# Attention trunk on one core: compressed scores kept in PSUM until their row minimum is subtracted

## The chip, the core and the metric

The kernel runs on one core of a Trainium2 chip. The metric is the device time of one execution in microseconds (us). The engines are named as in the profile: PE (TensorE, matrix products and transposes), ACT (ScalarE, activations and copies), DVE (VectorE, elementwise operations and reductions), POOL (GpSimd, elementwise operations, and it issues some DMAs), SP (it issues most DMAs).

## The reference

One layer of a decoder trunk over 512 positions of width 1024, in float32. A pooling mixer and a sparse attention with 16 heads of 64, in two key groups, are merged by gates and followed by a squared-ReLU MLP. The attention has three branches; the change touches the first, in which every query attends to 31 compressed keys per group:

```python
k_cmp = compress(kc.reshape(B, S, G, dh), pe_k, w_ck1, w_ck2)
v_cmp = compress(vc.reshape(B, S, G, dh), pe_v, w_cv1, w_cv2)
...
s_c = jnp.einsum('bqghd,bngd->bghqn', qb, k_cmp) * scale
p_c = masked_softmax(s_c, cmp_end[None, :] <= t[:, None])
o_c = jnp.einsum('bghqn,bngd->bqghd', p_c, v_cmp)
...
s_s = jnp.einsum('bqghd,bgqkd->bghqk', qb, k_sel) * scale
p_s = masked_softmax(s_s, ok[:, :, None])
...
o = gb[..., 0:1] * o_c + gb[..., 1:2] * o_s + gb[..., 2:3] * o_w
```

The other two branches (selected blocks, sliding window) are causal attention over all keys at these sizes, with keys of their own.

## The kernel before

Every float32 product is made of three products of rounded parts (high and low), so PE does about three times the plain work. The span has three stages: projections and the pooling mixer (to about 182 us), attention (about 182 to 390 us), and the output projections and the MLP.

**The attention stage.** Heads are worked in eight pairs. A pair has twelve slots: four in which both dense branches of one block of 128 queries are done together (`half == 0`), and eight with one branch each. Keys are negated beforehand, so the softmax works with a minimum and `exp(-x)`. A loop runs over all slots, each with steps for several engines:

- `score_pe` (L1013, PE): the scores of one slot, into a PSUM bank of the tag "S", which has three banks (`S_BANKS = 3`). `psS` is its name.
- `smax` (L1035, DVE): adds the mask, writes `P` in SBUF, takes the row minimum into `sm`.
- `expo` (L1045, ACT): the exponential, with row sums.
- `weight` (L1055 on DVE, a reciprocal; L1058 on POOL): scales `P` by reciprocal and gate.
- `turn_pe` (L1075, PE), four slots later: transposes `P` into a PSUM bank of the tag "T", of which there are two. `turn_hi` (L1086, ACT) and `turn_lo` (L1090, DVE) split it into `PT`.
- `pv` (L1109, PE): the product with the values. `o_evac` (L1116, L1118) takes it out.

**Compressed scores.** `cmp_scores(p)` does the compressed branch of the pair `p`, one pair ahead, as a generator whose steps run between the slots. Its PSUM tile `psC` is also one of the three "S" banks. Eight small products (L950) fill it: for each of 8 rows (4 query blocks x 2 heads) 32 high and 32 low columns. DVE adds the mask to the high part (L957) and the low part to that (L958), both into the SBUF tile `cw`; it takes the minimum over each row (L960) and subtracts it (L962), `cw` from `cw`. ACT takes the exponential (L965), DVE sum and reciprocal (L967, L968, L970), POOL scales and splits (L972, L974, L975), PE transposes (L983), ACT copies to `pc` (L985).

**Work between.** `fill2` does the remaining projections in `fm` (L394, PE). Their weights are split into a high part by ACT (L351) and a low part by DVE or POOL (L353). Queries are rotated in `rope`: ACT copies the projection to `rx` (L618), SP issues four DMAs that make `rs`, the same with halves swapped (L621), POOL multiplies both by tables (L626, L629), DVE adds them (L634), and `q_done` splits the sum into `Q` (L659 to L664).

**The order.** The source gives an emission order; a scheduler then orders the instructions of each engine by its own estimates of times, and puts semaphore waits in. Banks of a tag are handed out in turn: the tile that is asked for third after `psC` gets the bank of `psC`, and has to wait for the last reader of `psC`. That tile is the second of two scores 512 wide (128 queries x 512 keys) in a pair.

Of the kernel before, what the change touches and what calls it, by code (L numbers as in the profile page):

```python
# [16 lines left out]
ALU = mybir.AluOpType  # L17
AX = mybir.AxisListType
# [44 lines left out]
def trunk(ctx: ExitStack, tc: tile.TileContext, A, out):  # L63
    nc = tc.nc
    PE, ACT, DVE, POOL = nc.tensor, nc.scalar, nc.vector, nc.gpsimd
    PSUM = bass.MemoryType.PSUM

    def pool(name, **kw):
        return tc.tile_pool(name=name, bufs=1, reuse_waits="tile", **kw)
# [409 lines left out]
    op = e2.enter_context(pool("op"))  # L479
# [410 lines left out]
    with ExitStack() as c2:  # L890
# [54 lines left out]
        def cmp_scores(p):  # L945
            g = p // 4
            ps = ps2.tile([128, NT, 2, 64], F32, tag="S", bufs=S_BANKS, name="psC")
            for qb in range(NT):
                for h in range(2):
                    PE.matmul(ps[:, qb, h, :], Q[p][:, h, 128 * qb:128 * qb + 128], KC[g], start=True, stop=True,  # L950
                              skip_group_check=True)
            w = p2.tile([128, NT, 2, 64], F32, tag="cw", bufs=1, name="cw")
            s8 = p2.tile([128, 3, 8], F32, tag="c8", bufs=1, name="c8")
            cm = cst[:, C_CM:C_CM + 128].rearrange("p (q n) -> p q n", q=NT)
            wl = w[:, :, :, 0:32]
            wf = w.rearrange("p q h n -> p (q h) n")[:, :, 0:32]
            DVE.tensor_tensor(wl, ps[:, :, :, 0:32], cm[:, :, None, :].to_broadcast([128, NT, 2, 32]), op=ALU.add)  # L957
            DVE.tensor_tensor(wl, ps[:, :, :, 32:64], wl, op=ALU.add)  # L958
            yield
            DVE.tensor_reduce(s8[:, 0, :], wf, axis=AX.X, op=ALU.min)  # L960
            yield
            DVE.tensor_tensor(wf, wf, s8[:, 0, :, None].to_broadcast([128, 8, 32]), op=ALU.subtract)  # L962
            yield
            yield
            ACT.activation(wl, wl, AF.Exp, scale=-1.0)  # L965
            yield
            DVE.tensor_reduce(s8[:, 1, :], wf, axis=AX.X, op=ALU.add)  # L967
            DVE.reciprocal(s8[:, 2, :], s8[:, 1, :])  # L968
            r = s8[:, 2, :].rearrange("p (q h) -> p q h", q=NT)
            DVE.tensor_tensor(r, r, GT[:, :, 6 * p:6 * p + 6:3], op=ALU.mult)  # L970
            yield
            POOL.tensor_tensor(wl, wl, r[:, :, :, None].to_broadcast([128, NT, 2, 32]), op=ALU.mult)  # L972
            pH, pL = (PC[:, :, e, :].rearrange("p q (h n) -> p q h n", h=2) for e in range(2))
            POOL.tensor_scalar(pH, wl, 1.0, 1.0, op0=ALU.mult, op1=ALU.mult)  # L974
            POOL.tensor_tensor(pL, wl, pH.bitcast(F32), op=ALU.subtract)  # L975
            yield
            yield
            yield
            yield
            pt = ps2.tile([128, S], F32, tag="T", bufs=T_BANKS, name="psT")  # L980
            for qb in range(NT):
                src = PC[:, qb, :, :].rearrange("p e c -> p (e c)")
                PE.transpose(pt[:, 128 * qb:128 * qb + 128].bitcast(FR), src, identR)  # L983
            t = p2.tile([128, S], FR, tag="pc", bufs=1, name="pc")
            ACT.activation(t, pt, AF.Copy)  # L985
            PTc[p] = t
# [126 lines left out]
        def o_evac(p, half):  # L1113
# [7 lines left out]
            split_ready()  # L1121

        side.append(cmp_scores(0))
        while 0 not in PTc:
            fill()
            step_side()
        n = len(slots)
# [4 lines left out]
        for i in range(n + LAG + PLAG):  # L1132
            if i < n:
                p = slots[i][0]
                if i % 12 == 3 and p + 1 < NPAIR:
                    while p + 1 not in Q:
                        fill()
                        step_side()
                if i % 12 == CMP_AT and p + 1 < NPAIR:
                    side.append(cmp_scores(p + 1))  # L1140
# [51 lines left out]
    def bank():  # L1192
        return ps3.tile([128, S], F32, tag="B", bufs=8, name="psB")
# [396 lines left out]
    ps = [bank() for _ in range(2)]  # L1590
# [15 lines left out]
    for t in (2, 3):  # L1606
        n = 512 if t == 2 else 256
        for c in range(0, 512, n):
            ps = bank()[:, 0:n]
# [42 lines left out]
```

## Time and profile before

| | us |
|---|---|
| median of 3 runs | 816.5 (815.71 to 817.32) |
| profiled execution, its own time | 814.65 |
| span of the profiled execution | 812.9 |
| PE busy | 788.6 (97%) |
| DVE busy | 627.4 (77%) |
| ACT busy | 491.6 (60%) |
| POOL busy | 207.8 (26%) |

The span lies within the execution's time; 1.75 us of it are outside the span. Busy shares are means over stages that differ, so stages are read by themselves. In a row of the timeline the first number is the start, the second the time that the row covers, `x3` that three like instructions follow one another, and the brackets tell how long the engine was idle before it and what ended that. The granted clock (PEclk) is 1.00 at full speed.

### The profile page before, as it was taken

The numbers are of one execution on the slowest core, as the hardware profiler recorded it, in microseconds if no ns is written. First come the engines' busy times: TensorE is split into PE (matmuls) and PEld (weight loads), VectorE is DVE, ScalarE is ACT, GpSimd is POOL, SyncE is SP. The second block draws the span as 40 slices with busy tenths as digits, with TensorE's granted clock in tenths as the row PEclk, the third lists the DMA queues.
The fourth block names the chain that finished last, engine by engine and source line by source line (L and its number), as shares of the span: only waits on it lengthen the run. The fifth ranks groups of instructions, "written<-read, shape, count | busy, mean of one in ns | idle before, by whom it ended". The sixth has DMA issues, their size and how long they took to land.

```text
span 812.9 us, 14154 instructions
## 1 busy us (share of the span) xinstructions
PE 788.6 (97%) x5163; PEld 710.2 (87%) x5163; DVE 627.4 (77%) x1217; ACT 491.6 (60%) x968; POOL 207.8 (26%) x273
## 2 busy tenths in 40 slices
PE   8999999998899999999999999999999999999996
PEld 7889878886788888888788899999999999999996
DVE  5796744539879898889664579996889688978975
ACT  6576533337777888899434466943773477347833
POOL 4000000028766867665334100111111110000000
PEclk9999999999999999999999999999999999999999
DMA  9554633357446634553964707999998997754522
GB/s 304 143 158 122 164 92 94 102 170 153 67 124 122 144 79 92 104 131 65 328 152 154 202 9 208 311 243 283 250 286 218 285 266 194 222 164 156 181 79 104
DMA packets 128752, 136.65 MB, mean 168 GB/s; under 512 B 5349, under 2 KB 117001, under 8 KB 128522
## 3 DMA queue, kind: packets, MB, share of 16 engines
q1 hardware_dynamic: 107274, 113.98, 43.5%
q0 software_dynamic: 21120, 20.97, 18.1%
q8 instruction: 41, 0.67, 0.3%
q10 hardware_dynamic: 288, 0.79, 0.3%
q14 instruction: 29, 0.24, 0.1%
HBM read 131.01 MB, written 44.04 MB: 215 GB/s over the span
## 4 chain that ended last, share of the span: by engine, by line
PE 73%; DVE 16%; ACT 6%; issue 3%; DMA 1%; POOL 1%; ACTq 0%; DVEq 0%; POOLq 0%
PE psF L394 22%; PE psB L1379 15%; PE psB L394 12%; PE psB L1498 9%; PE psO L1109 3%; PE psT L1075 3%; PE psS L1013 2%; DVE wl L308 2%; PE psV L394 2%; DVE P L1035 2%; DVE PT L1090 1%; PE psF L451 1%; ACT P L1045 1%; DVE w3l L308 1%; PE psC L714 1%
## 5 line engine op out<-in xcount | busy, mean ns | idle before, releaser
L394 PE MATMUL psF<-R,wh 128*128 128x512 f32 x512 | 166.8, 404 | 0.9 <-ACT GB L688 0.6
L306 ACT ACTIVATE wh<-raw 128x1024 fp32r<-128x1024 f32 x70 | 74.0, 1057 | 74.5 <-PE psB L1498 32.6
L351 ACT ACTIVATE wh<-raw 128x512 fp32r<-128x512 f32 (+1 forms) x100 | 60.2, 620 | 82.2 <-PE psF L394 37.4
L394 PEld LDWEIGHTS psF<-R,wh 128*128 128x128 f32 x512 | 92.5, 189 | 18.7 <-ACT GB L688 0.8
L273 POOL DMA_DIRECT2D S<-w_ff x40 | 46.3, 1158 | 233.0 <-DMA S<-w_ff 162.5
L394 PE MATMUL psF<-R,wl 128*128 128x512 f32 x256 | 101.9, 398 | 0.8 <-DVE wl L353 0.8
L1058 POOL TENSOR_SCALAR P<-P,sm,GT 128x128 f32<-128x128 f32 (+3 forms) x128 | 85.7, 702 | 47.9 <-DVE sm L1055 34.1
L308 DVE TENSOR_TENSOR wl<-raw,wh 128x1024 fp32r<-128x1024 f32 x70 | 85.3, 1220 | 16.0 <-ACT wh L306 15.9
L353 DVE TENSOR_TENSOR wl<-raw,wh 128x512 fp32r<-128x512 f32 (+1 forms) x74 | 53.5, 734 | 32.9 <-ACT wh L351 32.5
L1045 ACT ACTIVATE P<-P,sm 128x128 f32<-128x128 f32 (+3 forms) x128 | 71.1, 557 | 12.1 <-DVE sm L1035 10.8
L1035 DVE CUSTOM_DVE_ANT_0 P<-psS,cst 128x128 f32<-128x128 f32 (+3 forms) x128 | 59.6, 483 | 6.2 <-PE psT L1075 4.6
L1379 PE MATMUL psB<-R,wh 128*128 128x256 f32 x352 | 64.1, 282 | 0.0
L353 POOL TENSOR_TENSOR wl<-raw,wh 128x512 fp32r<-128x512 f32 x28 | 39.0, 1398 | 87.6 <-ACT wh L351 85.2
L306 ACT ACTIVATE w3h<-raw 128x1024 fp32r<-128x1024 f32 x35 | 37.0, 1057 | 39.0 <-PE psB L1498 16.5
L1090 DVE TENSOR_TENSOR PT<-psT,PT 128x512 fp32r<-128x512 f32 (+2 forms) x96 | 56.6, 594 | 4.6 <-ACT PT L1086 3.5
L1086 ACT ACTIVATE PT<-psT 128x512 fp32r<-128x512 f32 (+2 forms) x96 | 49.3, 521 | 15.8 <-PE psT L1075 15.1
L394 PEld LDWEIGHTS psF<-R,wl 128*128 128x128 f32 x256 | 48.3, 188 | 11.8 <-DVE wl L353 0.9
L1075 PE MATMUL psT<-ident,P 128*128 128x128 f32 x320 | 51.6, 276 | 6.4 <-POOL P L1058 5.0
L1075 PEld LDWEIGHTS psT<-ident,P 128*128 128x128 f32 x320 | 40.2, 142 | 17.0 <-POOL P L1058 7.8
L308 DVE TENSOR_TENSOR w3l<-raw,w3h 128x1024 fp32r<-128x1024 f32 x35 | 42.7, 1221 | 15.2 <-ACT w3h L306 15.2
L1379 PEld LDWEIGHTS psB<-R,wh 128*128 128x128 f32 x352 | 54.1, 189 | 0.3 <-DVE R L1321 0.2
L1379 PE MATMUL psB<-R,wl 128*128 128x256 f32 x176 | 49.5, 281 | 0.0
(385 smaller groups left out, 2303.6 us busy)
## 6 DMA issues: line engine op xcount, KB each, us to landing
raw<-w_ff SPq DMA_DIRECT2D x55, 512.0 KB, 5.0
S<-w_ff POOLq DMA_DIRECT2D x40, 512.0 KB, 7.5
raw<-S SPq DMA_DIRECT2D x40, 512.0 KB, 5.1
raw<-w_in SPq DMA_DIRECT2D x32, 512.0 KB, 4.0
S<-w_ff SPq DMA_DIRECT2D x30, 512.0 KB, 5.6
S<-S SPq DMA_DIRECT2D x10, 512.0 KB, 6.6
raw<-w_proj_nsa SPq DMA_DIRECT2D x8, 512.0 KB, 4.1
raw<-w_out SPq DMA_DIRECT2D x8, 512.0 KB, 4.4
```

What stands on the lines that cost most here:

```text
L306: ACT.activation(h, t, AF.Copy)
L308: DVE.tensor_tensor(l, t, h.bitcast(F32), op=ALU.subtract)
L351: ACT.activation(h[:, sl], t[:, sl], AF.Copy)
L353: eng.tensor_tensor(l[:, sl], t[:, sl], h[:, sl].bitcast(F32), op=ALU.subtract)
L394: PE.matmul(ps, a, b, start=first and j == 0, stop=last and j == n - 1, skip_group_check=True)
L1035: DVE.tensor_tensor_reduce(out=P[:, o:o + n].rearrange("p (a c) -> p a c", c=128), in0=s, in1=m, scale=1.0, scalar=3e38, op0=ALU.add, op1= ...
L1045: last_exp[:] = [ACT.activation(c, c, AF.Exp, bias=sm[:, 0, e:e + 1], scale=-1.0, accum_out=sm[:, 1, e:e + 1])]
L1058: r = POOL.tensor_scalar(P[:, o:o + n], P[:, o:o + n], sm[:, 2, e:e + 1], GT[:, qb, c + e:c + e + 1], op0=ALU.mult, op1=ALU.mult)
L1075: PE.transpose(pt[:, 128 * j:128 * j + 128], P[:, 128 * j:128 * j + 128], ident)
L1090: DVE.tensor_tensor(dL, src, dH.bitcast(F32), op=ALU.subtract)
L1379: PE.matmul(out, w[u][:, k, 128 * f:128 * f + 128], XB[x][v][:, k, :], **kw)
L1498: PE.matmul(out, YB[y][u][:, k, 128 * f:128 * f + 128], w[v][:, k, :], **kw)
```

## The change

The sum of high and low part (L958) is now written back into `psC` in PSUM, no longer into `cw`. The minimum (now L961) and the subtraction (now L962) read it there; only the result of the subtraction goes to `cw`. The two are emitted directly one behind the other, where a `yield` stood between, and a `yield` is added behind them, so that all later steps are emitted where they were. The number and the shapes of the instructions are the same. Lines after L957 move by one.

```diff
             DVE.tensor_tensor(wl, ps[:, :, :, 0:32], cm[:, :, None, :].to_broadcast([128, NT, 2, 32]), op=ALU.add)
-            DVE.tensor_tensor(wl, ps[:, :, :, 32:64], wl, op=ALU.add)
-            yield
-            DVE.tensor_reduce(s8[:, 0, :], wf, axis=AX.X, op=ALU.min)
-            yield
-            DVE.tensor_tensor(wf, wf, s8[:, 0, :, None].to_broadcast([128, 8, 32]), op=ALU.subtract)
+            sc = ps.rearrange("p q h n -> p (q h) n")[:, :, 0:32]
+            DVE.tensor_tensor(ps[:, :, :, 0:32], ps[:, :, :, 32:64], wl, op=ALU.add)
+            yield
+            DVE.tensor_reduce(s8[:, 0, :], sc, axis=AX.X, op=ALU.min)
+            DVE.tensor_tensor(wf, sc, s8[:, 0, :, None].to_broadcast([128, 8, 32]), op=ALU.subtract)
+            yield
             yield
             yield
             ACT.activation(wl, wl, AF.Exp, scale=-1.0)
```

## The prediction, made before the changed kernel ran

> **What bounds the kernel now.** I read the page first, then busy time and granted clock by stretches, then PE's waits, then the timelines of PE, POOL and DVE where PE waits.
>
> ```profile
> PE 788.6 (97%) x5163; PEld 710.2 (87%) x5163; DVE 627.4 (77%) x1217; ACT 491.6 (60%) x968; POOL 207.8 (26%) x273
> ...
> 190.00:210.00 20.00, 16.25 (x98) 13.34 (x96) 18.16 (x52) 13.68 (x37) 14.34 (x21) 0.91 0.62 99
> 210.00:230.00 20.00, 17.44 (x109) 15.32 (x109) 17.86 (x52) 14.75 (x39) 14.38 (x22) 0.91 0.29 47
> 400.00:500.00 100.00, 99.22 (x532) 84.62 (x531) 66.65 (x90) 49.23 (x89) 22.24 (x17) 1.00 0.53 152
> ...
> 195.10:198.50 3.40, 2.78 (x10) 2.28 (x10) 2.86 (x10) 2.01 (x6) 2.70 (x4) 0.50 0.43 154
> 219.00:222.40 3.40, 3.40 (x15) 3.13 (x14) 2.95 (x9) 1.83 (x5) 2.16 (x4) 0.50 0.02 5
> ...
> PE psT L1075 <- POOL P L1058: 5.0, 3, 2.5
> PE psT L1075 <- DVE PT L1090: 0.6, 1, 0.6
> ACT cw L965 <- DVE cw L962: 4.8, 2, 3.3
> ```
>
> The columns of a stretch are its length, then PE, PEld, DVE, ACT and POOL busy, granted clock, DMA. PE bounds the kernel, so time is to be had only where PE is idle or slow. It loses 3.75 us from 190 to 210 and 2.56 from 210 to 230 (20.00 less 16.25 and 17.44). Each loss is followed by 3.4 us at clock 0.50, which cost half of PE's busy time in them: 1.4 and 1.7 us. I call the two places the first and the second jam.
>
> ```profile
> 189.22 4.16 DVE L962 TENSOR_TENSOR cw<-cw,c 128x256 f32<-128x256 f32 x1
> 193.92 1.03 DVE L634 TENSOR_TENSOR rx<-rx,rs 128x256 f32<-128x256 f32 x2
> 194.94 0.67 DVE L1090 TENSOR_TENSOR PT<-psT,PT 128x512 fp32r<-128x512 f32 x1
> 214.47 2.79 DVE L962 TENSOR_TENSOR cw<-cw,c 128x256 f32<-128x256 f32 x1
> ...
> 189.23 1.83 POOL L626 TENSOR_TENSOR rx<-rx,cst 128x256 f32<-128x256 f32 x2
> 190.63 1.78 POOL L629 TENSOR_TENSOR rs<-rs,cst 128x256 f32<-128x256 f32 x2
> 192.02 2.31 POOL L1058 TENSOR_SCALAR P<-P,sm,GT 128x256 f32<-128x256 f32 x3
> ...
> 192.98 0.44 PE L1075 MATMUL psT<-ident,P 128*128 128x128 f32 x2 [2.16 <-POOL P L1058]
> 217.72 0.96 PE L1075 MATMUL psT<-ident,P 128*128 128x128 f32 x4 [2.47 <-POOL P L1058]
> ...
> L958 DVE TENSOR_TENSOR cw<-psC,cw x8: 408/419/425, 172.9 to 341.6; 128x256 f32<-128x256 f32 x8
> L960 DVE TENSOR_REDUCE c<-cw x8: 398/407/421, 173.3 to 342.1; 128x8 f32<-128x256 f32 x8
> L962 DVE TENSOR_TENSOR cw<-cw,c x8: 412/571/4160, 173.8 to 343.2; 128x256 f32<-128x256 f32 x8
> L634 DVE TENSOR_TENSOR rx<-rx,rs x10: 393/574/1552, 193.9 to 318.7; 128x256 f32<-128x256 f32 x10
> L1090 DVE TENSOR_TENSOR PT<-psT,PT x84: 404/612/694, 188.0 to 363.7; 128x512 fp32r<-128x512 f32 x42, 128x384 fp32r<-128x384 f32 x28, 128x256 fp32r<-128x256 f32 x14
> ```
>
> L962 stands in both jams. It takes 412 ns at best, but 4160 and 2790 there, while POOL works without a gap. L634, which also takes both inputs from SBUF, is stretched to 1552 somewhere; L958 and L1090, of the same kind with one input from PSUM, never leave 408 to 425, and 694 for the longest form. So DVE is held where both inputs come from SBUF and POOL is working. That is the change's chance: its subtraction has one input in PSUM. But PE itself waits for POOL (L1058), and POOL was not held up by DVE in the first jam.
>
> **The change part by part.** *The three instructions.* L958 writes to PSUM, L960 and L962 read it. None of the rows has a DVE write to PSUM. Nearest are the three rows above: 398 to 425 ns with either kind of input, so I take no change, between -0.2 and +0.2 us for 24 instructions of which PE waits for few. [...]
>
> *The stall.* L962 falls to 0.42: 3.74 us of DVE time at the first jam, 2.37 at the second.
>
> *First jam.* POOL's order there is unchanged, and POOL has no gap from 189.23 on, so PE cannot go on before 192.98. Behind L962 DVE has one 512-wide L1035, then both L634. These need L629 (to about 191.3 and 192.0) and have both inputs in SBUF, so they inherit the hold. I let them end about 0.6 earlier than at 194.94 (bounds 0, if they are held as long as L962, and 2, if they run when L629 ends). L1090 behind them frees the bank for which PE waits 0.6 (the second row of the waits). Term: -0.6.
>
> *Second jam.* Here the scheduler moved more. On POOL, the split L353 that stands ahead of the rope is moved ahead of the four L1058 of 128:
>
> ```profile
> 208.80 0.89 POOL L1058 TENSOR_SCALAR P<-P,sm,GT 128x128 f32<-128x128 f32 x2 [1.33 <-DVE sm L1055]
> 211.36 1.09 POOL L1058 TENSOR_SCALAR P<-P,sm,GT 128x256 f32<-128x256 f32 x2 [0.47 <-DVE sm L1055]
> 213.08 1.78 POOL L353 TENSOR_TENSOR wl<-raw,wh 128x512 fp32r<-128x512 f32 x1
> 214.34 1.88 POOL L626 TENSOR_TENSOR rx<-rx,cst 128x256 f32<-128x256 f32 x2
> 216.43 1.76 POOL L1058 TENSOR_SCALAR P<-P,sm,GT 128x256 f32<-128x256 f32 x2
> 208.72 2.41 SPq L621 DMA_DIRECT2D rs<-rx  x4
> rs<-rx SPq DMA_DIRECT2D x4, 64.0 KB, 3.0
> ```
>
> L353 held POOL 1.26 (213.08 to 214.34); moved, it falls into idle time (1.33 and 0.47 in the brackets). L626 overwrites `rx`, which the four DMAs of SP read: the last is issued at about 210.6 and lands 3.0 later, 213.6. So L626 starts 0.74 earlier, not 1.26. The two L1058 at 216.43 took 1.76 where the same two at 211.36 took 1.09: 0.67 was L962's hold in the other direction. The sum would be 1.4; as L634 may collide there now, I take -1.2 (bounds 0 and -2.47, the whole wait). Two L394 are also moved ahead of the waiting transposes, at 0.23 each (rows below): -0.45. What is late next is the `rx` DMA.
>
> *The clock.* With the second wait shortened by 1.65 to 0.8, I expect no slow stretch there: -1.7 (bound 0). The wait of 0.76 that DVE's L353 causes up to 234.09 was followed by none, the clock stays at 1.00:
>
> ```profile
> 234.09 0.50 PE L394 MATMUL psF<-R,wl 128*128 128x512 f32 x1 [0.76 <-DVE wl L353]
> 234.42 0.63 PE L394 MATMUL psF<-R,wh 128*128 128x512 f32 x2
> 234.89 0.40 PE L394 MATMUL psF<-R,wl 128*128 128x512 f32 x1
> ...
> 234.00:236.00 2.00, 1.92 (x8) 1.60 (x9) 2.00 (x5) 0.48 (x3) 1.18 (x1) 1.00 0.32 77
> ```
>
> (From 234.42 to 234.89 two L394 are done, 0.23 each.) In the first jam I leave the 1.4 lost. [...]
>
> *The bank.* `psC` now holds its "S" bank until L962, not L958, and the second 512-wide L1013 of a pair waits for it. In pair 1 that is from 187.71 (first row below) to about 189.64 (189.22 and 0.42); PE has two L394 moved ahead, and the rest (1.4) only takes the place of waiting before 192.98. It costs nothing while POOL covers it, 1.4 if not. In pair 4 L962 ends at 271.06, 0.95 before that score starts; in pairs 3, 6 and 7 the rows are alike, with 0.9 to 1.3. In pair 5 (the last three rows) it does not:
>
> ```profile
> 187.71 0.47 PE L1013 MATMUL psS<-KH,Q 128*128 128x512 f32 x1
> 270.53 0.53 DVE L962 TENSOR_TENSOR cw<-cw,c 128x256 f32<-128x256 f32 x1
> 272.01 0.40 PE L1013 MATMUL psS<-KH,Q 128*128 128x512 f32 x1
> 295.95 0.39 PE L1013 MATMUL psS<-KH,Q 128*128 128x512 f32 x1
> 295.66 0.55 DVE L1035 CUSTOM_DVE_ANT_0 P<-psS,cst 128x384 f32<-128x384 f32 x1
> 296.53 0.41 DVE L962 TENSOR_TENSOR cw<-cw,c 128x256 f32<-128x256 f32 x1
> ```
>
> L962 now stands right behind that L1035, ends at about 296.6, and PE waits 0.6: +0.6. "Directly one behind the other" holds in the emission only: in the order of DVE, one to three instructions stand between minimum and subtraction in all pairs but the first.
>
> *Sum.* -0.6 - 1.2 - 0.45 - 1.7 + 0.6 = -3.35. The profiled execution of 814.65 would become 811.3. It lies 1.85 under the median of 816.5, by which the kernels are compared; there it gives 813.15. From 400 us on PE is all but never idle (99.22 of the 100 us to 500, and much the same to 780), so nothing behind eats a gain.
>
> **The rivals.** *The wait moves on (no change).* L634 inherits the hold, the `rx` DMA lands later, POOL ends both jams when it did, and both slow stretches stay. For it: PE's large waits name POOL, not DVE. Against it: POOL's L353 is gone from the second jam by the order. Left are -0.6, -0.45 and +0.6: 816.1. It decides if POOL's L1058 of the second jam ends within 0.5 us of before.
>
> *The bank costs (slower).* One mechanism: the second 512-wide score of each pair waits for L962, and the transposes queued behind it on PE are late, then ACT's and DVE's splits, then L962 of the next pair. It decides if DVE falls behind PE by about 1.3 us (one 512-wide L1035 and L1090) more than here: then the waits are 0.0 to 0.4 in four pairs (about 0.8), 1.9 in pair 5, 2.7 in pair 1, 0.5 in pair 2 (where it now ends about when the score is due), together 5.9, less 3.35: +2.6, 819.1 (an estimate from these rows). Against it: L962 gives DVE 6.1 us (3.74 and 2.37).
>
> *Both jams go (faster still).* The wait split by the bank in the first jam no longer slows the clock (1.4 more), and pair 5 does not wait: -3.35 - 1.4 - 0.6 = -5.35, 811.15.
>
> **How the numbers follow.** No change can be told within 0.2%, 1.6 us, the spread of the runs shown. Forecast 0.45 (811.5 to 814.9 by its own terms), both jams go 0.13, no change 0.20, slower 0.22. Faster by over 0.2% means under 814.87: the forecast and the case beyond it, nearly all, and a little of the third: 0.59. Same 0.19, slower 0.22. The range goes from 810.0 (beyond the case at 811.15 by the unspent part of the second wait) to 819.1, with about 1 in 10 left out at each end.
>
> **What would show it.** L962 at 0.40 to 0.45 in all eight; L634 of the first jam stretched; PE's waits for POOL L1058 near 3.5 in sum, not 5.0; one stretch at clock 0.50 between 185 and 225, not two; a PE wait of L1013 for DVE in pair 5. It is wrong if L962 is still stretched, if POOL's L1058 of the second jam ends as late as before, or if L1013 waits in most pairs.

## The result

| executions | before, median us | changed, median us | ratio | 95% interval |
|---|---|---|---|---|
| the result the prediction was made for (6 and 6) | 816.11 | 811.76 | 0.9961 | 0.9948 to 0.9974 |
| repeat on a second chip (23 and 12) | 816.05 | 813.90 | 0.9977 | 0.9966 to 0.9989 |
| repeat on a third chip (17 and 12) | 817.02 | 813.94 | 0.9966 | 0.9953 to 0.9979 |

The ratio and its interval are those estimated from the single runs, and not the quotient of the two medians (0.9947 in the first row). The changed kernel is faster, by 2 to 4 us of 816; all three intervals lie below 1. The profiled execution took 811.65 us, its span 809.8 (before 814.65 and 812.9).

The first view of the changed kernel is the page's line of busy time, then busy time and granted clock by stretches, and the same for the two windows that showed clock 0.50 before (columns: length, PE, PEld, DVE, ACT, POOL, clock, DMA share, GB/s).

```profile
PE 788.0 (97%) x5163; PEld 709.1 (88%) x5163; DVE 621.4 (77%) x1217; ACT 491.3 (61%) x968; POOL 207.9 (26%) x273
...
190.00:210.00 20.00, 16.55 (x96) 13.40 (x95) 15.16 (x51) 13.58 (x36) 15.50 (x22) 0.91 0.62 100
210.00:230.00 20.00, 18.58 (x120) 15.83 (x119) 18.13 (x60) 15.95 (x44) 14.09 (x23) 1.00 0.28 47
...
195.10:198.51 3.41, 3.41 (x12) 2.82 (x12) 2.07 (x7) 1.79 (x5) 2.55 (x4) 0.50 0.61 163
219.00:222.41 3.41, 3.41 (x24) 3.02 (x23) 2.86 (x8) 2.45 (x8) 1.78 (x3) 1.00 0.01 2
```

PE's loss from 190 to 210 is 3.45 us (3.75 before), from 210 to 230 1.42 (2.56 before). The stretch at clock 0.50 behind the first jam is still there. The one behind the second jam is gone: in the same 3.4 us PE does 24 matmuls where it did 15.

Next come the operations of the change (minimum, median and maximum in ns), PE's waits from 165 to 400 us, and the timelines of DVE, PE and POOL in the two jams.

```profile
L959 DVE TENSOR_TENSOR psC<-psC,cw x8: 420/427/433, 172.8 to 338.7; 128x256 f32<-128x256 f32 x8
L961 DVE TENSOR_REDUCE c<-psC x8: 408/414/425, 173.3 to 339.2; 128x8 f32<-128x256 f32 x8
L962 DVE TENSOR_TENSOR cw<-psC,c x8: 405/412/424, 173.7 to 340.3; 128x256 f32<-128x256 f32 x8
L634 DVE TENSOR_TENSOR rx<-rx,rs x10: 397/722/1718, 191.7 to 316.1; 128x256 f32<-128x256 f32 x10
...
PE psT L1076 <- POOL P L1059: 4.0, 3, 2.2
PE psT L984 <- DVE PT L1091: 0.6, 1, 0.6
PE psF L394 <- DVE wl L353: 0.4, 1, 0.4
...
189.16 0.41 DVE L962 TENSOR_TENSOR cw<-psC,c 128x256 f32<-128x256 f32 x1
191.71 1.94 DVE L634 TENSOR_TENSOR rx<-rx,rs 128x256 f32<-128x256 f32 x2 [1.53 <-POOL rs L629]
193.64 0.67 DVE L1091 TENSOR_TENSOR PT<-psT,PT 128x512 fp32r<-128x512 f32 x1
192.93 0.44 PE L1076 MATMUL psT<-ident,P 128*128 128x128 f32 x2 [2.21 <-POOL P L1059]
193.94 0.44 PE L1076 MATMUL psT<-ident,P 128*128 128x128 f32 x2 [0.58 <-POOL P L1059]
216.93 0.96 PE L1076 MATMUL psT<-ident,P 128*128 128x128 f32 x4 [1.21 <-POOL P L1059]
208.06 1.29 POOL L353 TENSOR_TENSOR wl<-raw,wh 128x512 fp32r<-128x512 f32 x1 [0.66 <-ACT wh L351]
213.78 1.90 POOL L626 TENSOR_TENSOR rx<-rx,cst 128x256 f32<-128x256 f32 x2
215.89 1.50 POOL L1059 TENSOR_SCALAR P<-P,sm,GT 128x256 f32<-128x256 f32 x2
```

L962 is never held: 424 ns at most, against 4160. In the first jam POOL's run of rope instructions still decides when PE goes on (192.93, 192.98 before), and L634, the next DVE instruction with both inputs in SBUF, is the one now held (1602 ns there). In the second jam L353 has gone ahead of the four 128-wide L1059 and the rope, the two 256-wide L1059 for which PE waits end at about 217.39 instead of 218.19, and PE waits 1.21 instead of 2.47.

### The profile page after: what moved, and what is told of

Its sections match the earlier page's. It is cut to its first block, busy times and chain, and to the rows that moved or that the text cites. A ratio compares the mean times of both kernels' runs of the same rounds, so it can differ in the third digit from the quotient of the medians.

```text
span 809.8 us, 14149 instructions
## 1 busy us (share of the span) xinstructions
PE 788.0 (97%) x5163; PEld 709.1 (88%) x5163; DVE 621.4 (77%) x1217; ACT 491.3 (61%) x968; POOL 207.9 (26%) x273
## 4 chain that ended last, share of the span: by engine, by line
PE 75%; DVE 14%; ACT 5%; issue 3%; POOL 2%; DMA 1%; SPq 0%; ACTq 0%; DVEq 0%; POOLq 0%
PE psF L394 22%; PE psB L1380 15%; PE psB L394 12%; PE psB L1499 9%; PE psO L1110 3%; PE psT L1076 3%; PE psS L1014 3%; DVE wl L308 2%; PE psV L394 2%; PE psF L451 1%; DVE w3l L308 1%; PE psC L714 1%; DVE P L1036 1%; ACT wh L306 1%; POOL P L1059 1%
## 5 line engine op out<-in xcount | busy, mean ns | idle before, releaser
L394 PE MATMUL psF<-R,wh 128*128 128x512 f32 x512 | 166.6, 404 | 0.8 <-ACT GB L688 0.6
L306 ACT ACTIVATE wh<-raw 128x1024 fp32r<-128x1024 f32 x70 | 74.0, 1058 | 74.0 <-PE psB L1499 32.6
L394 PEld LDWEIGHTS psF<-R,wh 128*128 128x128 f32 x512 | 92.4, 189 | 19.0 <-ACT GB L688 0.9
L394 PE MATMUL psF<-R,wl 128*128 128x512 f32 x256 | 101.9, 398 | 0.4 <-DVE wl L353 0.4
L1059 POOL TENSOR_SCALAR P<-P,sm,GT 128x128 f32<-128x128 f32 (+3 forms) x128 | 86.0, 708 | 42.2 <-DVE sm L1056 28.7
L353 DVE TENSOR_TENSOR wl<-raw,wh 128x512 fp32r<-128x512 f32 (+1 forms) x74 | 53.5, 734 | 33.3 <-ACT wh L351 32.3
L1036 DVE CUSTOM_DVE_ANT_0 P<-psS,cst 128x128 f32<-128x128 f32 (+3 forms) x128 | 59.7, 484 | 6.8 <-PE psT L1076 5.1
L353 POOL TENSOR_TENSOR wl<-raw,wh 128x512 fp32r<-128x512 f32 x28 | 38.1, 1364 | 88.4 <-ACT wh L351 86.1
L306 ACT ACTIVATE w3h<-raw 128x1024 fp32r<-128x1024 f32 x35 | 37.0, 1056 | 39.2 <-PE psB L1499 17.0
L1091 DVE TENSOR_TENSOR PT<-psT,PT 128x512 fp32r<-128x512 f32 (+2 forms) x96 | 56.5, 594 | 3.4 <-ACT PT L1087 2.6
L394 PEld LDWEIGHTS psF<-R,wl 128*128 128x128 f32 x256 | 48.3, 189 | 11.4 <-DVE wl L353 0.6
```

Source lines behind the costliest of these rows:

```text
L306: ACT.activation(h, t, AF.Copy)
L353: eng.tensor_tensor(l[:, sl], t[:, sl], h[:, sl].bitcast(F32), op=ALU.subtract)
L394: PE.matmul(ps, a, b, start=first and j == 0, stop=last and j == n - 1, skip_group_check=True)
L1036: DVE.tensor_tensor_reduce(out=P[:, o:o + n].rearrange("p (a c) -> p a c", c=128), in0=s, in1=m, scale=1.0, scalar=3e38, op0=ALU.add, op1= ...
L1059: r = POOL.tensor_scalar(P[:, o:o + n], P[:, o:o + n], sm[:, 2, e:e + 1], GT[:, qb, c + e:c + e + 1], op0=ALU.mult, op1=ALU.mult)
L1091: DVE.tensor_tensor(dL, src, dH.bitcast(F32), op=ALU.subtract)
```

## The experiments

Ratios are to the kernel before, run on the same chip, and are estimated as above. The medians of before were 815.36 for the first four rows (35 runs), 816.05 for the next three (23), 817.02 for the last (17).

| kernel | runs | median us | ratio | 95% interval |
|---|---|---|---|---|
| scores in PSUM, old places | 12 | 814.00 | 0.9982 | 0.9970 to 0.9994 |
| adjacent, scores in SBUF | 12 | 815.36 | 0.9997 | 0.9984 to 1.0010 |
| bank held, scores in SBUF | 12 | 815.26 | 1.0005 | 0.9993 to 1.0016 |
| changed, ropes later | 12 | 817.49 | 1.0027 | 1.0015 to 1.0038 |
| before, rope on DVE | 12 | 813.68 | 0.9971 | 0.9958 to 0.9985 |
| changed, rope on DVE | 6 | 812.50 | 0.9957 | 0.9943 to 0.9972 |
| changed, early ropes later | 6 | 811.97 | 0.9949 | 0.9934 to 0.9964 |
| changed, two ropes on DVE | 6 | 811.07 | 0.9935 | 0.9918 to 0.9952 |

**Is it the place in PSUM or the place in the code?** Two kernels each do one half of the change. The first keeps the scores in PSUM and the old yield between minimum and subtraction:

```diff
             DVE.tensor_reduce(s8[:, 0, :], sc, axis=AX.X, op=ALU.min)
+            yield
             DVE.tensor_tensor(wf, sc, s8[:, 0, :, None].to_broadcast([128, 8, 32]), op=ALU.subtract)
-            yield
```

> The scores stay in PSUM as in the changed kernel, but minimum and subtraction are emitted at their old places (a yield between them). Theory A (what counts is where the operands lie: L962 is no longer held, and psC keeps its bank longer, which makes the scheduler put POOL's L353 ahead of four L1058 in the second jam): as the changed kernel, 0.995 to 0.997 of before, 811.5 to 813; L962 0.41 in all eight, PE waits 1.2 and not 2.5 for POOL near 217, no clock of 0.50 behind it. Theory B (it is the place directly behind the minimum that counts): no gain, 0.999 to 1.001, about 816.

The second puts the two directly one behind the other, with the scores in `cw` as before:

```diff
             DVE.tensor_reduce(s8[:, 0, :], wf, axis=AX.X, op=ALU.min)
-            yield
             DVE.tensor_tensor(wf, wf, s8[:, 0, :, None].to_broadcast([128, 8, 32]), op=ALU.subtract)
+            yield
```

> Minimum and subtraction directly one behind the other, the scores in SBUF as before. Theory A (operands): about as before, 0.999 to 1.001; L962 still stretched to some 4 and 2.8 us in the two jams, PE's waits for POOL 5.0 us in sum and two stretches at clock 0.50. Theory B (adjacency): 0.996, L962 outside POOL's run and not stretched.

The first came out at 0.9982, the changed kernel itself at 0.9961, 0.9977 and 0.9966: intervals that overlap. The second came out as before. The rows of its subtraction (L961 there) and of PE's waits:

```profile
190.47 4.14 DVE L961 TENSOR_TENSOR cw<-cw,c 128x256 f32<-128x256 f32 x1
213.84 3.67 DVE L961 TENSOR_TENSOR cw<-cw,c 128x256 f32<-128x256 f32 x1
194.23 1.45 PE L1075 MATMUL psT<-ident,P 128*128 128x128 f32 x4 [2.17 <-POOL P L1058]
218.04 0.69 PE L1013 MATMUL psS<-KH,Q 128*128 128x384 f32 x1 [2.62 <-DVE sm L1035]
```

The hold is as long as before in the first jam and longer in the second (3.67 to 2.79), where PE now waits for DVE. Adjacency alone gives nothing; the operand in PSUM gives the gain. What adjacency adds once the operand lies there is within the noise of these runs. My expectation of the first kernel missed in two points: 0.9982 is less of a gain than the 0.995 to 0.997 that I gave, and its profiled execution still had a stretch at clock 0.50 behind the second jam, after a wait of 1.56.

**The order, or the hold?** A longer held bank made the scheduler move POOL's L353. This kernel holds the bank by an added one-column copy, and keeps the subtraction in SBUF:

```diff
             DVE.tensor_reduce(s8[:, 0, :], wf, axis=AX.X, op=ALU.min)
-            yield
             DVE.tensor_tensor(wf, wf, s8[:, 0, :, None].to_broadcast([128, 8, 32]), op=ALU.subtract)
+            DVE.tensor_copy(s8[:, 2, 0:1], ps[:, 0, 0, 0:1])
+            yield
```

> Scores, minimum and subtraction in SBUF as before, minimum and subtraction adjacent, and an added DVE copy of one column of psC behind the subtraction (about 0.1 us, eight times; it isn't used), so that psC keeps its bank as long as in the changed kernel and the scheduler moves POOL's L353 ahead of the 128-wide L1058, while L962 has both inputs in SBUF. Theory A1 (the moved L353 brings the second jam's gain): PE's wait there 2.47 to about 1.5, perhaps without the stretch at clock 0.50: 0.996 to 0.998, 813 to 814.5, with L962 still stretched to over 2 us. Theory A2 (the hold of L962 is what counts, the order doesn't): 0.999 to 1.001, 815.5 to 817.

The scheduler put the copy (0.14 us) ahead of the subtraction on DVE (213.89 and 214.43 in the second jam), but it did move L353. The timelines of POOL, DVE and PE at that jam:

```profile
207.56 1.30 POOL L353 TENSOR_TENSOR wl<-raw,wh 128x512 fp32r<-128x512 f32 x1 [0.66 <-ACT wh L351]
215.55 1.52 POOL L1059 TENSOR_SCALAR P<-P,sm,GT 128x256 f32<-128x256 f32 x2
214.43 3.61 DVE L961 TENSOR_TENSOR cw<-cw,c 128x256 f32<-128x256 f32 x1
218.03 0.40 DVE L1091 TENSOR_TENSOR PT<-psT,PT 128x256 fp32r<-128x256 f32 x1
218.58 0.63 PE L1076 MATMUL psT<-ident,P 128*128 128x128 f32 x4 [2.76 <-DVE PT L1091]
```

L353 is moved and POOL is done as early as in the changed kernel, but DVE is held until 218.04, L1091 behind it comes late, and PE waits 2.76. So the moved L353 doesn't pay without the freed DVE; whether the freed DVE would pay without the moved L353 was not run. The total (1.0005) fits A2, but it is not a clean measure: PE is idle 1.5 us longer from 250 to 290, mostly in waits for DVE's `oT` (0.97 and 0.87), and the mean granted clock of its runs, 0.9967 to 0.9941, means that some 2 us of slow clock were saved and lost again elsewhere.

**Is POOL's run of rope instructions the cause of the jams?** In `rope` both kernels get `eng = DVE`, so that L626 and L629 leave POOL:

```diff
-        eng = POOL if mode["pool"] else DVE
+        eng = DVE
```

> The kernel before with the two rope multiplications (L626, L629) on DVE and not on POOL, so that POOL has no unbroken run in the two jams. If the run of rope instructions on POOL is what makes the jams (L962 held, PE waiting for POOL's L1058): L962 not over 1.0 us anywhere, PE's waits for POOL between 185 and 225 us 5.0 to under 2.5, at most one stretch at clock 0.50: 0.994 to 0.998, 810.5 to 813.7. If DVE has no room for 16 to 28 more instructions of some 0.4 us there, its waits take their place: 0.999 to 1.002.

> The changed kernel with the same two multiplications on DVE. If the change's gain is that L962 is no longer held by POOL's run, nothing of it is left once the run is gone: within 1 us of the same edit in the kernel before, either way. If the gain lies in the order that the longer held bank brings, it stays 2 to 4 us under that one.

```profile
L962 DVE TENSOR_TENSOR cw<-cw,c x8: 406/410/424, 174.9 to 342.2; 128x256 f32<-128x256 f32 x8
190.00:210.00 20.00, 19.57 (x127) 16.27 (x126) 19.25 (x66) 17.20 (x48) 16.76 (x23) 1.00 0.76 122
```

These are rows of the kernel before with the rope on DVE. Its subtraction still has both inputs in SBUF and is never longer than 424 ns, and PE's waits for POOL between 185 and 225 are gone: the hold comes from POOL's run. It missed on the clock: in the profiled execution, the slowest of the twelve, two stretches at 0.50 stood at 230.9 and 326.4, behind waits that the kernel before doesn't have. Its time is 0.9971, beside 0.9977 for the changed kernel on the same chip, so this one line in `rope` is worth about as much as the change. With both, the ratio is 0.9957: between my two forecasts, 1.2 us in the medians below the edit alone, with intervals that overlap.

**Can the first jam go too?** Six yields ahead of L626, first for all ropes from the pairs on, then only while `scored["pairs"] < 2`; at last, without yields, the ropes of that time on DVE:

```diff
-        eng = POOL if mode["pool"] else DVE
+        for _ in range(6 if mode["pool"] else 0):
+            yield
+        eng = POOL if mode["pool"] else DVE
```

> The changed kernel with six more yields ahead of the two rope multiplications on POOL (L626, L629), so that in the first jam the 256-wide L1058 (1059 here) stand between and ahead of them and PE isn't kept waiting for four rope instructions in a row. Theory A (in the first jam POOL's unbroken run is what PE waits for, and the wait of 2.2 us is what brings the stretch at clock 0.50 behind it): the wait falls below 1 us, the slow stretch (1.4) goes: 2 to 3.5 us under the changed kernel, 808 to 810, ratio to before 0.991 to 0.993. Rival (the rope instructions become late themselves: L634, L1091 behind it and then PE's scores wait as long): as the changed kernel or slower, 811.5 to 814.

> The changed kernel with six more yields ahead of the rope multiplications in the first jam alone, not in the later ones, where they had cost waits of 1.2, 1.0 and 2.6 us near 246, 255 and 285 us. If these waits came from the later ropes being late, they go and the gain in the first jam (wait 2.2 to about 1.0, no stretch at clock 0.50) is left: 1.5 to 3 us under the changed kernel, 809 to 810.5. If they come from the first one's lateness: still 815 to 817.

```diff
-        eng = POOL if mode["pool"] else DVE
+        eng = POOL if mode["pool"] and scored["pairs"] >= 2 else DVE
```

> The changed kernel with the rope multiplications of the first jam alone on DVE. If the first jam is POOL's run of four rope instructions and DVE has room there (it idles 1.5 us waiting for L629): PE's waits between 189 and 196 fall from 2.8 to under 0.5 us, no stretch at clock 0.50, and the second jam stays as in the changed kernel: 809.5 to 811.5, ratio 0.993 to 0.995 (with weights that land late, to 0.996). If the transposes then wait for DVE as long: as the changed kernel, 0.996 to 0.998.

All three took the stretch at clock 0.50 out of the first jam. With all ropes later, PE's wait for `oT` at 246.70 and 254.94 (1.17 and 0.96) and one of 2.61 at 285.18 took its place, the latter with a stretch at clock 0.50 behind it: 1.0027, slower than either of my forecasts. With only the early ones later, the one for `sm` at 285 went (0.91 for `pc` was left there), those for `oT` stayed, against my forecast: 0.9949, 1.9 us under the changed kernel on the same chip. The last one is the best kernel of the study, 0.9935, and 2.9 us under the changed kernel on the same chip (811.07 to 813.94). Its edit reached the ropes of both jams, not of the first alone as I had expected; PE's waits from 185 to 225 are two of 0.2, and no stretch at clock 0.50 is left before the end:

```profile
PE psT L1076 <- DVE PT L1091: 0.2, 1, 0.2
PE psS L1014 <- DVE sm L1036: 0.2, 1, 0.2
```

**What chance does between executions.** Before and the changed kernel were profiled again, before twice:

> The changed kernel itself, beside the three below and before. If minimum and subtraction being emitted together matters little once the scores lie in PSUM, the ratio is near that of the run with the old places, 0.997 to 0.9985 (813 to 814); if it is worth something, 0.995 to 0.9965 (811.3 to 812.5). Of the gain some 1.4 us should be clock: a mean granted clock of 0.996 against 0.994.

> The kernel before once more, for one profiled execution. From the end of PE's 1.7 us wait for mH (near 395 us) to the end of the span it took 417.3 us in the first one; of ten profiled executions of eight kernels five took 417.1 to 417.8 and five 418.9 to 419.7. If weights that land late eat a gain made ahead of them, before, which comes to this point latest, keeps to the lower group; if it is chance per execution, either. Clock: stretches at 0.50 behind the first, the second, both or none of the jams, as the grid of 3.41 us falls; about three in four each.

> The kernel before a third time, for another profiled execution: the same two questions (417.1 to 417.8 or 418.9 to 419.7 from the wait for mH to the end; which of the two jams has a stretch at clock 0.50 behind it).

> The changed kernel a third time. If later weights eat part of the gain: 418.9 to 419.7 from the wait for mH to the end, more often than before. The wait for POOL near 217 is 1.2, as in its other two executions, and no stretch at clock 0.50 stands behind it wherever the grid falls (PE is busy for 2.1 of the 3.41 us at the least); behind the first jam one stands in about four of five. Ratio 0.996 to 0.9985.

All three executions of before have a stretch at 0.50 at both jams; all three of the changed kernel have one behind the first alone. Over all timed executions the mean granted clock was 0.9941 for before (75) and 0.9963 for the changed kernel (30): 0.0022 of 812 us is 1.8 us, one stretch of 3.4 us at half clock.

The end of PE's wait for mH marks the end of the attention stages. Its rows in before, the changed kernel and its third execution, then PE's busy time from 500 to 600 in the same three, and the first L306 after 490 that waits for a weight of `w_ff` (before, then third execution):

```profile
395.61 0.70 PE L394 MATMUL psB<-R,wh 128*128 128x512 f32 x2 [1.67 <-ACT mH L1279]
392.73 0.70 PE L394 MATMUL psB<-R,wh 128*128 128x512 f32 x2 [1.67 <-ACT mH L1280]
393.17 0.70 PE L394 MATMUL psB<-R,wh 128*128 128x512 f32 x2 [1.67 <-ACT mH L1280]
...
500.00:600.00 100.00, 98.97 (x828) 98.39 (x828) 85.55 (x101) 61.11 (x82) 11.56 (x10) 1.00 1.00 272
500.00:600.00 100.00, 98.99 (x828) 98.41 (x827) 86.66 (x102) 62.33 (x86) 11.56 (x10) 1.00 1.00 274
500.00:600.00 100.00, 98.02 (x816) 97.03 (x815) 84.05 (x99) 60.26 (x82) 11.56 (x10) 1.00 1.00 269
...
503.09 1.06 ACT L306 ACTIVATE wh<-raw 128x1024 fp32r<-128x1024 f32 x1 [1.29 <-DMA raw<-w_ff]
504.04 1.06 ACT L306 ACTIVATE wh<-raw 128x1024 fp32r<-128x1024 f32 x1 [3.32 <-DMA raw<-w_ff]
```

Up to the mark the gain is 2.6 us (means of three executions each, 395.5 and 392.9). From the mark to the end of the span before took 417.3, 418.3 and 417.6, the changed kernel 417.1, 419.0 and 419.9: on the mean 0.9 is given back, about half of it in waits of PE, none of which is over 0.7 us. The weight of the last two rows is split 107.5 us after the mark in before and 110.9 in the third execution of the changed kernel. Whether an earlier mark makes this likelier or chance alone does it, three executions each can't tell; it stays open. Two other kernels speak against the mark as the only cause: with the bank held it stood at 395.1, with the rope on DVE at 394.6, as late as in before, and the rest took 419.4 and 419.7.

## Why the prediction held, step by step

**L962 freed: right.** The forecast was 0.40 to 0.45 in all eight; it is 405 to 424 ns. Cost of the three instructions: 7 or 8 ns more for L959 and L961 by their medians (427 to 419, 414 to 407), and nothing to be seen in L962 (405 ns at best, 412 before). The hold goes with the place of the operands: in the two jams the subtraction took 4.14 and 3.67 us with two inputs in SBUF (adjacent, scores in SBUF), 0.41 and 0.42 with one (changed kernel).

**First jam, -0.6: right in kind, too large.** L634 inherits the hold, as written, and ends at 193.64, 1.3 earlier; the wait of 0.62 for L1090 is gone. But the second wait for POOL grew from 0.34 to 0.58. PE's waits in the jam sum to 2.79 instead of 3.12: -0.3. Even that isn't shown over executions: in the third execution of before, whose slow stretch began at 193.09, the two short waits are missing and the sum is 2.16.

**Second jam and the two L394, -1.2 and -0.45: the size was off.** I forecast a wait shortened by 1.65 to 0.8; it is 1.21 to 1.23 in the three executions, shortened by 1.25. L626 starts 0.56 earlier (0.74 forecast), but not for my reason. I had the `rx` DMA land at 213.6, from the last issue and the median landing; in the traces the semaphores of its four parts were complete at 212.63 in before and at 212.53 in the changed kernel. Rows of the changed kernel: what POOL does just ahead of L626 at 213.78, and when its sequencer was through with L626's waits for the DMA:

```profile
212.03 1.09 POOL L1059 TENSOR_SCALAR P<-P,sm,GT 128x256 f32<-128x256 f32 x2 [0.96 <-DVE sm L1056]
213.07 1.14 POOL L273 DMA_DIRECT2D S<-w_ff  x1
L626 POOLq EVENT_SEMAPHORE  x2: 17/30/43, 212.5 to 212.6; - x2
```

POOL has no gap before L626. What holds it is POOL's own queue: these two L1059 start 0.67 later than before (212.03 to 211.36), for DVE now does a 384-wide L1036 ahead of their reciprocal. Of the 1.26 that the moved L353 frees, 0.6 is left; that it came near my 0.74 is luck. The two L1059 for which PE waits took 1.50 where I assumed 1.09: of the 0.67 that I had put down to L962's hold, 0.26 went.

**Clock, -1.7: right in size, not in reason.** The mean clock says 1.8, and each execution shows it. But it isn't the length of a wait that decides: a stretch at clock 0.50 followed one of 1.56 (old places) and none followed one of 2.76 (bank held), see below.

**Bank, +0.6 and 1.4 covered: wrong.** No wait of a score for DVE's L962 is in the list of waits. In pair 5 I set L962 behind the L1035 that began at 295.66, with a 512-wide score to wait for it:

```profile
293.40 0.42 DVE L962 TENSOR_TENSOR cw<-psC,c 128x256 f32<-128x256 f32 x1
293.54 0.50 PE L1014 MATMUL psS<-KH,Q 128*128 128x512 f32 x1
295.61 0.34 PE L1014 MATMUL psS<-KH,Q 128*128 128x384 f32 x1
```

The 512-wide score starts at 293.54 while L962 still runs, so it isn't the one that waits for the bank; the next, 384 wide, comes 1.8 after the end of L962. In pair 1 likewise a 384-wide one stands behind L962 now. In the new order no score has to wait; I had taken the order of before with L962 alone put elsewhere.

**"Nothing behind eats a gain": only partly right.** PE is busy for 98 to 99 of 100 us there, but in some executions of the changed kernel weights are late there, and 0.9 of the 2.6 is lost on the mean, of which chance may be a part (above).

The sum was -3.35 and the measured differences of the medians are -4.35, -2.15 and -3.08. Two misses cancel: the bank's wait of 0.6 that wasn't there, and first jam and second jam together 0.7 smaller than forecast. Of the terms as measured (-0.3, -1.25, -1.7, together -3.25) only 2.6 arrive at the mark. The stretch from the first L950 to the mark, in before and the changed kernel, shows where the rest goes:

```profile
171.39:395.61 224.22, 213.38 (x1316) 184.07 (x1314) 188.07 (x591) 177.68 (x466) 149.04 (x203) 0.98 0.52 116
171.32:392.73 221.41, 212.68 (x1315) 182.85 (x1314) 182.52 (x591) 177.47 (x466) 149.20 (x203) 0.99 0.53 117
```

On the mean of three executions each, PE's idle time there falls from 10.4 to 9.0, and what half clock costs its work (half of the busy time in the slow stretches) from 3.2 to 1.7. But the rest of PE's busy time, for the same matmuls in another order (the counts differ by one at the edge of the window), grows from 210.2 to 210.8: together -2.4, and 0.2 of the 2.6 arose ahead of the first L950, where the kernels don't differ. The other two kernels that hold the bank longer have 210.7 (old places) and 211.5 (bank held), the one with adjacency alone 210.2. So the longer held bank seems to cost about 0.6 after all, not as the wait that I had forecast but in PE's order of work; that the size is alike is luck, and which matmuls cost it was not settled. Of the rivals, "the bank costs" and "the wait moves on" are out by the waits. "Both jams go" didn't happen, for the first stretch at 0.50 stayed; the two ropes on DVE show what it is worth.

## What to carry to other kernels

An instruction of 0.4 us that takes 4 us in one place is worth a look at where its operands lie and what the neighbouring engine does at that moment; here moving one operand freed it (4.16 to 0.41 us), and so did moving the neighbour's run of work (0.42 at most). That paid only as far as the next engine's queue allowed: the freed DVE was worth something in the jam where POOL's order changed as well (PE's wait 2.47 to 1.21), and little where POOL's own run bound PE (its waits 3.12 to 2.79). Taking that run itself off POOL is a one-line edit: for all ropes, in the kernel before, it was worth about as much as the change; for two ropes, on top of the change, another 2.9 us.

## What the hardware showed beyond that

The stretches at clock 0.50 ahead of the last microseconds lie on a grid of 3.41 us that runs through an execution: in each of the three of before the two stretches start 23.9 us apart, seven windows. Its position is not the same in all three (the first stretch at 195.10, 195.79 and 193.09). PE's busy time in the window ahead of a stretch, in rows of before (two windows), the changed kernel (the same two) and the kernel with the bank held (all its four windows at the jams; it had no stretch at 0.50 before the end):

```profile
191.69:195.10 3.41, 1.77 (x8) 1.05 (x8) 3.41 (x7) 1.49 (x4) 2.64 (x5) 1.00 0.76 121
215.58:219.00 3.42, 1.20 (x7) 0.87 (x8) 3.38 (x7) 1.00 (x3) 3.42 (x6) 1.00 0.77 122
191.69:195.10 3.41, 1.59 (x9) 1.06 (x9) 3.33 (x8) 0.60 (x1) 3.41 (x5) 1.00 0.73 115
215.58:219.00 3.42, 2.13 (x14) 1.67 (x14) 2.26 (x7) 1.89 (x5) 3.42 (x7) 1.00 0.92 143
...
189.56:192.97 3.41, 1.73 (x12) 1.22 (x9) 3.41 (x2) 0.90 (x3) 3.41 (x6) 1.00 0.68 76
192.97:196.39 3.42, 2.04 (x10) 1.30 (x11) 3.42 (x8) 1.71 (x4) 2.43 (x4) 1.00 0.49 78
213.46:216.87 3.41, 2.36 (x15) 1.76 (x13) 3.41 (x6) 2.39 (x7) 3.41 (x7) 1.00 1.12 275
216.87:220.28 3.41, 1.70 (x13) 1.65 (x14) 3.37 (x9) 1.34 (x3) 1.66 (x4) 1.00 0.56 89
```

The windows with 1.77, 1.20 and 1.59 were followed by a stretch, the others not. In all 14 profiles every window from 160 us on with PE busy for up to 1.62 was followed by one, none with 1.9 or more, and between 1.65 and 1.81 it went either way: in these traces PE must be busy for about half of a window. So a wait of 2.76, split between two windows, cost no clock in the kernel with the bank held, and one of 1.56 did in the kernel with the old places. Sliding the grid over the traces, a window under 1.7 turns up in about three of four positions at each jam of before, and in none at the second jam of the changed kernel (2.1 at the least). The length of the window and the half that decides are read from these traces alone.
